# Weight remainders of three projections by an accumulating DMA in a hybrid decoder block

## The chip, the cores and the metric

The kernel runs on one core of a Trainium2 chip. The metric is the device time of one execution in microseconds (us). The engines of the core work side by side: TensorE (PE, with its weight loads as PEld), VectorE (DVE), ScalarE (ACT), GpSimd (POOL) and SyncE (SP), which in this kernel issues the transfers. Data come from HBM into SBUF, and TensorE writes its results to PSUM.

## The reference

One decoder layer on 512 tokens of width 1024, in float32. Cut to what matters:

```
h = rms_norm(x, g_pre_mix) * (1 + scale1) + shift1          # shift, scale, gate = silu(c) @ w_ada + b_ada
z = h @ w_in                                                # 2048 GLU | 384 q | 256 kv | 64 rope key | 2 x 1024 gates
u = ua * sigmoid(ub)
u = silu(layer_norm(causal_depthwise_conv(u, conv_w, conv_b)))   # 31 taps, 1024 channels
y_a = u @ w_conv_out
q, kv = rms_norm(q_lat) @ w_uq, rms_norm(kv_lat) @ w_ukv
y_b = attention(q, kv, rope) @ w_attn_out                   # 8 heads, causal
y = (sigmoid(g_a) * y_a + sigmoid(g_b) * y_b) @ w_out
x = x + gate1 * rms_norm(y, g_post_mix)
h = rms_norm(x, g_pre_mlp) * (1 + scale2) + shift2
x = x + gate2 * rms_norm(relu(h @ w_mlp_in)**2 @ w_mlp_out, g_post_mlp)
```

## The kernel before, in words

**Three matmuls for one.** TensorE multiplies in a rounded float format (fp32r). To keep float32 accuracy each factor is split into a rounded high part h and a remainder l = value - h, and a product is made of three matmuls: h*h, h*l and l*h (`mm3`). For activations the split is made as they leave PSUM. For weights, class `W` (line 470) makes it: ACT copies the float32 weights to the rounded high part, then DVE subtracts that from the weights to make the remainder.

**Weight units.** `wunit` (line 490) loads a block of weights of at most 128 x 1024 words (512 KB) from HBM into a buffer of the float arena `f_arena`, splits it into two buffers of the arena `r_arena`, and frees the float buffer. A unit of 1024 columns feeds 24 matmuls of 512 columns. Both arenas are one long SBUF tensor each (22,400 and 28,000 words per partition), in which places are given and taken back, so how far ahead weights are prepared depends on the room.

**The stages.** First the norm of x, the modulation from `w_ada`, and the first products with `w_in` (seven column blocks, whose weights go through `W` directly). Then the latents (`lat_gemm`, line 818), the rest of the GLU columns (`glu_tile`, line 898) and the latent norm; the attention, head by head; the projection `w_attn_out`, then the two gates (`C_GB`, then `C_GA`, columns of `w_in`) and `w_conv_out`, all four through `feat_gemm` (line 1152) in groups of output tiles; `w_out`, and the MLP with a Strassen scheme.

**The convolution** runs on DVE: 8 channel tiles of 31 taps, in pairs of tiles (0,1), (2,3), (4,5), (6,7). A tap is one instruction of 128 x 512 that reads the padded input and the accumulator, both in SBUF. Taps have no other consumer than the LayerNorm over channels, so they fill DVE's free time from 73 to 371 us. The LayerNorm's statistics (`ln_stats`, line 1214) begin with tiles 0 to 3: TensorE transposes them for one token tile, ACT sums them, POOL scales the sum, and ACT squares the transposed values with that as bias, after which the PSUM bank is free for the next token tile:

```
act.activation(ra.v(j), pb.v(b, n * P), AF.Copy, accum_out=sA[:, t:t + 1])
pool.tensor_scalar(ns[:, t:t + 1], sA[:, t:t + 1], -1.0 / (n * P), None, ALU.mult)
...
act.activation(ra.v(j), pb.v(b, n * P), AF.Square, bias=ns[:, t:t + 1], accum_out=q[:, t:t + 1])
```

They are recorded behind the gate `C_GB`, with a high rank for TensorE.

**The order.** Nothing is issued as it is written. A planner records all operations with their dependences, gives each an assumed cost (475 ns on the issuing engine for a DMA, then a shared DMA resource with fixed latencies), and simulates the engines: TensorE takes the ready operation of the lowest rank, every other engine the one that is due first. The order that comes out is written to the engines' queues, where each engine then works strictly in that order. The arenas' places are planned over several passes, and the pass with the shortest simulated length is taken. So a change of one operation can shift the order of others. In the profile nearly every instruction has line 388, at which the planner issues; groups are told apart by tiles.

Of the kernel before, what the change touches and what calls it, by code (L numbers as in the profile page):

```python
# [15 lines left out]
ALU = mybir.AluOpType  # L16
# [376 lines left out]
def tile_hybrid_block(  # L393
# [12 lines left out]
    out = out[0]  # L406
    w_ada, w_in, conv_w, w_conv_out = w_ada[0], w_in[0], conv_w[0], w_conv_out[0]
    w_uq, w_ukv, w_attn_out, w_out = w_uq[0], w_ukv[0], w_attn_out[0], w_out[0]
# [31 lines left out]
    def emit(past, replay):  # L440
        fa = Arena(FT, F_WORDS, past.get("f_arena"), replay.get("f_arena"))
        ra = Arena(RT, R_WORDS, past.get("r_arena"), replay.get("r_arena"))
        pb = Banks(PT, past.get("psum"), replay.get("psum"))
        plan = Planner(nc, dict(f_arena=fa, r_arena=ra, psum=pb))
        pe, act, dve, pool, sp = (plan.engine(e) for e in Planner.NAMES)

        def rf(b, pat=None, **kw):
            a = RTF[:, b[0]:b[0] + b[1]]
            return a.rearrange(pat, **kw) if pat else a
# [12 lines left out]
        def pair(words):  # L462
            return ra.alloc(words), ra.alloc(words)

        def load(words, src, pat=None, **kw):
            b = fa.alloc(words)
            sp.dma_start(out=fa.v(b, pat, **kw), in_=src)
            return b

        class W:  # L470


            def __init__(self, src, a, b):
                self.a, self.b = a, b
                self.h, self.l = pair(a * b)
                act.copy(ra.v(self.h, "p (a b) -> p a b", a=a), src)
                dve.tensor_tensor(ra.v(self.l, "p (a b) -> p a b", a=a), src,
                                  rf(self.h, "p (a b) -> p a b", a=a), ALU.subtract)

# [10 lines left out]
        def wunit(src, k0, c0, nk, nc_):  # L490

            wb = load(nk * nc_, src[k0 * P:(k0 + nk) * P, c0:c0 + nc_].rearrange("(k p) n -> p k n", p=P),
                      "p (k n) -> p k n", k=nk)
            w = W(fa.v(wb, "p (k n) -> p k n", k=nk), nk, nc_)
            fa.free(wb)
            return w

# [3 lines left out]
        def stat(n=1):  # L501
            a = st_n[0]
            st_n[0] += n
            assert st_n[0] <= 96
            return st[:, a:a + n]
# [36 lines left out]
        for t in range(NT):  # L542
            b = fa.alloc(D)
# [7 lines left out]
        for i, vecs in enumerate(((("bada", b_ada), ("gpm", g_pre_mix)),  # L551
# [5 lines left out]
            for nm, src in vecs:  # L557
                n = src.shape[1] // P
# [40 lines left out]
        for t in range(NT):  # L599
            j = ra.alloc(D)  # L600
            s = stat(2)
# [7 lines left out]
        for k in range(KD):  # L609
            b = pb.alloc()  # L610
# [77 lines left out]
        for ks in KGRP:  # L688
            plan.hurry = HA - 1e4 * ks[0]
            n = len(ks) * P  # L690
# [127 lines left out]
        def lat_gemm():  # L818
            lb = [pb.alloc() for _ in range(NT)]
            for k0 in range(0, KD, 2):  # L820
                w = wunit(w_in, k0, C_QL, 2, 512)
                for k in range(2):
                    for t in range(NT):
                        mm3(pb.v(lb[t]), hs(k0 + k, t * P, P), w(k, 0, 512), k0 + k == 0, k0 + k == KD - 1)
                w.free()
                pump(PUMPS[0])
            for t in range(NT):
                b = fa.alloc(640)
                act.copy(fa.v(b)[:, 0:512], pb.v(lb[t]))
                latF.append(b)  # L830
            pb.free(*lb)
            ws = [wunit(w_in, kh, C_R2, 4, 192) for kh in (0, 4)]
            for t in range(NT):
                b = pb.alloc()
                for k in range(KD):
                    mm3(pb.v(b, 192), hs(k, t * P, P), ws[k // 4](k % 4, 0, 192), k == 0, k == KD - 1)
                act.copy(fa.v(latF[t])[:, 512:640], pb.v(b, 128))
                act.copy(fa.v(kraw)[:, t * DR:(t + 1) * DR], pb.v(b, 192)[:, 128:192])
                pb.free(b)
            for w in ws:  # L840
                w.free()
            pump(PUMPS[0])
# [55 lines left out]
        def glu_tile(ct, s, n):  # L898

            bb = [pb.alloc() for _ in range(n)]  # L900
            for kh in range(0, KD, 4):
                w = wunit(w_in, kh, s * D + ct * P, 4, n * P)
                for o in range(n):
                    for k in range(4):
                        mm3(pb.v(bb[o]), w(k, o * P, P), hs(kh + k), kh + k == 0, kh + k == KD - 1)
                w.free()
            return bb
# [433 lines left out]
        for t in range(NT):  # L1341
            b = fa.alloc(D)
# [8 lines left out]
        for k0 in range(0, KD, 2):  # L1351
            w = wunit(w_out, k0, 0, 2, 512)
# [16 lines left out]
        for tp in range(2):  # L1369
            xn = []  # L1370
            for t in (2 * tp, 2 * tp + 1):
# [4 lines left out]
                s = stat(6)  # L1376
# [26 lines left out]
            for k2 in range(KD // 2):  # L1403
                b = pb.alloc()
                for q in range(2):
                    for t in range(2):
                        k = 2 * k2 + q
                        pe.transpose(pb.v(b)[:, (2 * q + t) * P:(2 * q + t + 1) * P], fa.v(xn[t])[:, k * P:(k + 1) * P], ident)
                for q in range(2):
                    k = 2 * k2 + q  # L1410
# [223 lines left out]
```

## Time and profile before

| what | us |
|---|---|
| median of 3 runs (lowest to highest) | 838.59 (838.47 to 839.24) |
| profiled execution | 836.4 |
| its span | 834.6 |
| PE busy | 808.1 |
| DVE busy | 685.2 |
| ACT busy | 415.5 |
| POOL busy | 45.4 |

The span is the time from the first to the last instruction; the profiled execution is 1.8 us longer. Busy times are sums over the span, and they say nothing about who waits for whom; for that the profile has a chain of waits, a timeline, and groups of instructions with the idle time before them. In a group's row stand engine, operation, what is written from what (tile names), partitions x elements and types, the count, the busy time, the mean length in ns, and the idle time before with what ended it.

### The profile page before, as it was taken

How to read it: one execution, taken by the hardware profiler on the slowest of the kernel's cores; microseconds unless marked ns; L12 is line 12 of the kernel's file. 1: busy time of each engine (PE TensorE's matmuls, PEld its weight loads, DVE VectorE, ACT ScalarE, POOL GpSimd, SP SyncE). 2: the span in 40 equal slices, each digit the busy share in tenths (PEclk: the TensorE clock that was granted, in tenths of full speed). 3: DMA queues.
4: the chain of work that ended last, by engine and by line, in shares of the span. 5: the costliest groups of instructions: out<-in, count | busy, mean ns of one | idle time of the engine just before them, and what ended most of it. 6: DMA issues, size and time to landing. Idle time of an engine off the chain costs nothing.

```text
span 834.6 us, 10659 instructions
## 1 busy us (share of the span) xinstructions
PE 808.1 (97%) x3940; PEld 675.7 (81%) x3940; DVE 685.2 (82%) x1012; ACT 415.5 (50%) x680; POOL 45.4 (5%) x119
## 2 busy tenths in 40 slices
PE   6999999999999989999999989999999999999995
PEld 3777888899988868888888779888888888888884
DVE  4979979999999997999999779298529993975696
ACT  5463363375893346227434287375346544553641
POOL 3001040000000020000000230000000000000002
PEclk9999999999999999999999989999999999999998
DMA  9997423202353141332799650064014831660302
GB/s 310 336 311 234 148 69 98 67 27 77 101 177 102 51 128 49 101 111 91 233 353 363 210 201 27 26 202 152 0 51 132 290 132 51 197 206 1 101 1 101
DMA packets 86823, 117.28 MB, mean 141 GB/s; under 512 B 7274, under 2 KB 60627, under 8 KB 86770
## 3 DMA queue, kind: packets, MB, share of 16 engines
q1 hardware_dynamic: 86770, 116.59, 43.5%
q8 instruction: 31, 0.51, 0.2%
q14 instruction: 22, 0.18, 0.1%
HBM read 108.18 MB, written 8.39 MB: 140 GB/s over the span
## 4 chain that ended last, share of the span: by engine, by line
PE 85%; DMA 4%; DVE 3%; POOL 2%; issue 2%; ACT 2%; SPq 1%; DVEq 0%; POOLq 0%; ACTq 0%
PE psum L388 85%; DMA f_arena<-in_w_in_dram 4%; DVE f_arena L388 3%; SPq L388 1%; POOL stats L388 1%; ACT f_arena L388 1%; DMA f_arena<-in_x_dram 1%; ACT r_arena L388 1%; POOL lns L388 1%; DVE r_arena L388 0%; DVEq L1629 0%; POOLq L1629 0%; DMA rows<-in_kv_norm_g_dram 0%; DVE mod L388 0%; DVE cols L388 0%
## 5 line engine op out<-in xcount | busy, mean ns | idle before, releaser
L388 PE MATMUL psum<-r_arena 128*128 128x512 f32 (+2 forms) x3592 | 766.5, 374 | 4.0 <-ACT r_arena L388 2.5
L388 PEld LDWEIGHTS psum<-r_arena 128*128 128x128 f32 x3592 | 634.4, 190 | 121.0 <-ACT r_arena L388 3.6
L388 DVE TENSOR_TENSOR r_arena<-f_arena,r_arena 128x1024 fp32r<-128x1024 f32 (+4 forms) x232 | 247.9, 1090 | 97.1 <-PE psum L388 48.5
L388 ACT CAST r_arena<-f_arena 128x1024 fp32r<-128x1024 f32 (+4 forms) x222 | 209.7, 966 | 183.3 <-PE psum L388 111.5
L388 DVE SCALAR_TENSOR_TENSOR f_arena<-f_arena,cw 128x512 f32<-128x512 f32 x240 | 164.8, 743 | 0.0
L388 ACT ACTIVATE f_arena<-psum 128x512 f32<-128x512 f32 x64 | 38.0, 597 | 119.6 <-PE psum L388 111.3
L388 DVE TENSOR_TENSOR f_arena<-f_arena 128x1024 f32<-128x1024 f32 (+3 forms) x78 | 77.0, 1003 | 8.3 <-ACT f_arena L388 6.3
L388 ACT ACTIVATE f_arena<-f_arena 128x512 f32<-128x512 f32 (+3 forms) x100 | 58.5, 604 | 20.2 <-DVE f_arena L388 19.4
L388 DVE SCALAR_TENSOR_TENSOR f_arena<-f_arena,cT 128x256 f32<-128x256 f32 (+2 forms) x84 | 55.2, 699 | 0.1
L388 PE MATMUL psum<-ident,f_arena 128*128 128x128 f32 (+1 forms) x240 | 35.3, 288 | 11.7 <-DVE f_arena L388 7.7
L388 PEld LDWEIGHTS psum<-ident,f_arena 128*128 128x128 f32 (+1 forms) x240 | 29.2, 148 | 17.2 <-DVE f_arena L388 8.7
L388 POOL TENSOR_SCALAR stats<-stats 128x1 f32<-128x1 f32 x32 | 14.8, 463 | 467.0 <-ACT r_arena L388 361.6
L388 DVE TENSOR_TENSOR f_arena<-psum,f_arena 128x512 f32<-128x512 f32 x52 | 35.2, 684 | 4.2 <-PE psum L388 3.9
L388 ACT CAST r_arena<-psum 128x512 fp32r<-128x512 f32 (+2 forms) x57 | 30.2, 566 | 15.8 <-PE psum L388 15.4
L388 DVE TENSOR_TENSOR r_arena<-psum,r_arena 128x512 fp32r<-128x512 f32 (+2 forms) x57 | 35.7, 656 | 2.2 <-ACT r_arena L388 1.9
L388 ACT COPY f_arena<-psum 128x512 f32<-128x512 f32 (+4 forms) x42 | 19.9, 500 | 23.0 <-PE psum L388 22.7
L388 ACT ACTIVATE r_arena<-f_arena 128x512 fp32r<-128x512 f32 (+3 forms) x20 | 13.0, 648 | 21.9 <-DVE f_arena L388 18.8
L388 DVE CUSTOM_DVE_ANT_0 f_arena<-psum,mask 128x128 f32<-128x128 f32 (+3 forms) x32 | 15.0, 484 | 2.5 <-PE psum L388 2.5
L388 POOL TENSOR_SCALAR lns<-lns 128x1 f32<-128x1 f32 x4 | 5.3, 1326 | 198.5 <-ACT r_arena L388 198.5
L388 POOL TENSOR_TENSOR stats<-stats,nhalf 128x1 f32<-128x1 f32 x24 | 15.2, 633 | 1.9
L388 DVE TENSOR_SCALAR f_arena<-f_arena,stats 128x1024 f32<-128x1024 f32 x8 | 6.0, 754 | 9.9 <-POOL stats L388 9.7
L388 DVE SCALAR_TENSOR_TENSOR f_arena<-f_arena 128x512 f32<-128x512 f32 (+1 forms) x18 | 13.1, 742 | 0.0
(93 smaller groups left out, 195.4 us busy)
## 6 DMA issues: line engine op xcount, KB each, us to landing
f_arena<-in_w_ada_dram SPq DMA_DIRECT2D x16, 1024.0 KB, 5.6
f_arena<-in_w_mlp_in_dram SPq DMA_DIRECT2D x32, 512.0 KB, 5.1
f_arena<-in_w_mlp_out_dram SPq DMA_DIRECT2D x32, 512.0 KB, 5.2
f_arena<-in_w_in_dram SPq DMA_DIRECT2D x28, 512.0 KB, 4.9
f_arena<-in_x_dram SPq DMA_DIRECT2D x8, 512.0 KB, 5.3
f_arena<-in_w_ada_dram SPq DMA_DIRECT2D x16, 256.0 KB, 5.7
f_arena<-in_w_ada_dram SPq DMA_DIRECT2D x8, 512.0 KB, 6.7
h_spill<-r_arena SPq DMA_DIRECT2D x16, 256.0 KB, 5.4
```

Source lines behind the costliest of these rows:

```text
L388: getattr(self.real[o.eng], o.fn)(*o.a, **o.k)
```

## The change

`W` gets a flag `by_dma`. With it, DVE's subtraction is left out. In its place ACT writes the negated weights, in the rounded format, into the remainder's buffer, and POOL issues a DMA from the float buffer to that buffer which adds what it carries to what lies there. `wunit` sets the flag where the source is `w_in`, `w_attn_out` or `w_conv_out`: 48 units, 44 of them of 1024 columns, two of 768 and two of 512. The weights of the first products, of `w_uq`, `w_ukv`, `w_out` and of the MLP are split as before.

```diff
-            def __init__(self, src, a, b):
+            def __init__(self, src, a, b, by_dma=False):
                 self.a, self.b = a, b
                 self.h, self.l = pair(a * b)
                 act.copy(ra.v(self.h, "p (a b) -> p a b", a=a), src)
+                if by_dma:
+                    act.mul(ra.v(self.l, "p (a b) -> p a b", a=a), src, -1.0)
+                    pool.dma_start(out=ra.v(self.l, "p (a b) -> p a b", a=a), in_=src, accum_op=ALU.add)
+                    return
                 dve.tensor_tensor(ra.v(self.l, "p (a b) -> p a b", a=a), src,
                                   rf(self.h, "p (a b) -> p a b", a=a), ALU.subtract)
...
-            w = W(fa.v(wb, "p (k n) -> p k n", k=nk), nk, nc_)
+            w = W(fa.v(wb, "p (k n) -> p k n", k=nk), nk, nc_, by_dma=any(src is s for s in (w_in, w_attn_out, w_conv_out)))
```

## The prediction

> **What bounds the kernel now.** I read the page's first part, the windows of 20 us, the chain that ended last, and then the timeline around the one place where the chain leaves TensorE in the stretch that the change touches.
>
> ```profile
> PE 808.1 (97%) x3940; PEld 675.7 (81%) x3940; DVE 685.2 (82%) x1012; ACT 415.5 (50%) x680; POOL 45.4 (5%) x119
> 280.00:300.00 20.00, 20.00 (x90) 16.57 (x89) 19.36 (x24) 10.27 (x12) 0.00 (x0) 1.00 0.38 108
> 300.00:320.00 20.00, 16.00 (x73) 12.73 (x72) 14.89 (x22) 8.93 (x23) 5.31 (x4) 0.91 0.25 78
> 247.31 58.80 PE psum L388 x262
> 306.90 4.63 POOL lns L388
> 312.39 69.46 PE psum L388 x312
> ...
> 312.40:320.00 7.60, 7.60 (x34) 6.19 (x34) 3.46 (x5) 5.74 (x17) 0.69 (x3) 0.78 0.26 71
> ```
>
> In the windows (the last row is one more) the columns are window and length, then busy us of PE, weight load, DVE, ACT and POOL, granted clock, DMA share and GB/s; in the chain they are start, length, and who. TensorE bounds the kernel. From 68 to 463 us, in which nearly all the changed weights are consumed, it has one break of over half a microsecond: the four idle microseconds of the 300:320 window. There the chain runs through a POOL instruction of the LayerNorm statistics. After the idle time the clock is low for a while (0.78 in the 7.6 us after it, 1.00 before), which costs another 7.6 x 0.22 = 1.7. The place is worth 5.7 us. DVE is nearly full in these windows, but TensorE does not wait for it.
>
> This is that place, in the timeline (start, length, engine, what, in brackets the idle time before and its releaser):
>
> ```profile
> 304.91 5.38 DVE L388 SCALAR_TENSOR_TENSOR f_arena<-f_arena,cw 128x512 f32<-128x512 f32 x8
> 305.85 2.54 PE L388 MATMUL psum<-r_arena 128*128 128x512 f32 x10
> 306.90 4.62 POOL L388 TENSOR_SCALAR lns<-lns 128x1 f32<-128x1 f32 x1 [191.51 <-ACT r_arena L388]
> 310.21 1.22 DVE L388 TENSOR_TENSOR r_arena<-f_arena,r_arena 128x1024 fp32r<-128x1024 f32 x1
> 312.39 0.81 PE L388 MATMUL psum<-ident,f_arena 128*128 128x128 f32 x5 [4.00 <-ACT r_arena L388]
> L388 POOL TENSOR_SCALAR lns<-lns x4: 207/240/4618, 306.9 to 318.9; 128x1 f32<-128x1 f32 x4
> ```
>
> The POOL instruction scales one number per partition, and its sisters take 0.2 us (the last row: shortest, median, longest). This one lasts 4.62 us and ends at 311.52, just after DVE's unbroken train of instructions with two SBUF inputs (convolution taps, then one weight remainder) ends at 311.43. The same happened earlier:
>
> ```profile
> 97.72 9.36 DVE L388 SCALAR_TENSOR_TENSOR f_arena<-f_arena,cw 128x512 f32<-128x512 f32 x14
> 105.42 1.71 POOL L388 TENSOR_SCALAR stats<-stats 128x1 f32<-128x1 f32 x1 [33.27 <-ACT r_arena L388]
> ```
>
> The train ends at 107.08, the POOL instruction at 107.13. So a POOL instruction that reads SBUF stands still until DVE's train breaks. It is decisive what breaks the train, and the change removes what does.
>
> **The change, part by part.** There are 48 weight units (w_in 32, attention output 8, convolution output 8); 44 have 1024 columns.
>
> Removed: 48 remainders on DVE, 44 of them of 1.22 us, some 57 us in all.
>
> ```profile
> L388 DVE TENSOR_TENSOR r_arena<-f_arena,r_arena 128x1024 fp32r<-128x1024 f32 x28 | 34.2, 1227 | 4.5 <-ACT r_arena L388 4.5
> f_arena<-in_w_ukv_dram SPq DMA_DIRECT2D x4, 512.0 KB, 4.3
> 305.00:371.00 66.00, 46.78 (x70) 0.97 0.21 64
> ```
>
> TensorE does not wait for them, so directly they are worth 0. Indirectly they move the convolution forward. The first row is DVE from 70 to 305 us: 28 remainders, of which the four of w_ukv stay, so 24 go. Inside a train each costs 1.13 us from start to start (259.44 to 260.57, below), so 27.1; their share of the waits for ACT, 24/28 of 4.5, is 3.9. DVE is 31.0 us ahead at 305.
>
> Added on ACT: 48 copies with factor -1, 44 of them at 1.06 us.
>
> ```profile
> L388 ACT ACTIVATE r_arena<-f_arena 128x1024 fp32r<-128x1024 f32 x4 | 4.2, 1056 | 2.8 <-DMA f_arena<-in_x_dram 2.8
> 64.34 1.06 ACT L388 CAST r_arena<-f_arena 128x1024 fp32r<-128x1024 f32 x1 [0.49 <-DMA f_arena<-in_w_in_dram]
> 65.30 1.56 ACT L388 ACTIVATE f_arena<-psum 128x512 f32<-128x512 f32 x3
> ```
>
> That is about 50 us on an engine at 50%: hidden, with one exception. At 57 to 66 us ACT also feeds the end of the first products, and the gate (65.30) stands behind weight copies. Up to four added copies there could delay it by 0 to 4.2 us. I take 0, since the gate has the earlier deadline.
>
> Added on POOL: 48 DMA issues, each waiting in order for its ACT copy. Behind them stand the memsets of the padded inputs, the latent norm's statistics and the four LayerNorm instructions above. No DMA of before is issued by POOL; SP's take 0.4 us, and a price matters only above 5.44 us, the spacing of the units (263.76 to 269.20 below). I take 0.
>
> Added on the DMA engines: 48 accumulating transfers.
>
> ```profile
> x_spill<-f_arena SPq DMA_DIRECT2D x4, 512.0 KB, 3.2
> f_arena<-in_w_out_dram SPq DMA_DIRECT2D x8, 512.0 KB, 6.6
> 263.76 1.05 ACT L388 CAST r_arena<-f_arena 128x1024 fp32r<-128x1024 f32 x1 [1.85 <-PE psum L388]
> 269.20 1.06 ACT L388 CAST r_arena<-f_arena 128x1024 fp32r<-128x1024 f32 x1 [3.91 <-PE psum L388]
> 264.72 0.57 ACT L388 COPY f_arena<-psum 128x512 f32<-128x512 f32 x1
> L388 ACT CAST r_arena<-f_arena 128x1024 fp32r<-128x1024 f32 x21 | 22.1, 1056 | 32.6 <-PE psum L388 32.6
> 415.62 1.05 ACT L388 CAST r_arena<-f_arena 128x1024 fp32r<-128x1024 f32 x1 [4.33 <-DMA f_arena<-in_w_conv_out_dram]
> 413.00 0.69 DVE L388 SCALAR_TENSOR_TENSOR f_arena<-f_arena,psum 128x512 f32<-128x512 f32 x1 [0.96 <-PE psum L388]
> ```
>
> Nothing of before accumulates. From below, 512 KB land 3.2 us after issue; from above I take twice 6.6, the slowest weight row, read two times: 13.2. The cover: between 252 and 345 us there are 21 casts (sixth row) for 24 units, so three units were cast before, and the cast at 263.76 is the sixth attention-output unit. The copy at 264.72 closes the second unit (at about 264.1 on TensorE), so the sixth is needed three units later, at 264.1 + 3 x 5.44 = 280.4. From the end of cast and added copy (265.9) that leaves 14.5 us, and both ends fit. At the convolution output the first group of four units ends at 413.0 + 3 x 1.36 = 417.1 (its four tiles close a quarter of 5.44 apart, and the first at 413.0), so the sixth unit is due at 422.5; its cast ends at 416.67, and with the copy 4.8 us are left. The lower price fits, the upper misses by 8.4. I take the lower: these casts wait for loads that wait for buffers, and with the convolution done earlier buffers come free earlier. An f_arena buffer is held some 4 us longer, at the same cover.
>
> **The sum.** At 305 us there were 70 taps left, 46.8 us (the row with x70, DVE's taps alone). DVE is 31.0 ahead, so the taps end at 305 + 46.8 - 31.0 = 320.8. What broke the train in before was a weight remainder waiting for its ACT copy, every 5.4 us:
>
> ```profile
> 259.44 1.22 DVE L388 TENSOR_TENSOR r_arena<-f_arena,r_arena 128x1024 fp32r<-128x1024 f32 x1
> 260.57 2.07 DVE L388 SCALAR_TENSOR_TENSOR f_arena<-f_arena,cw 128x512 f32<-128x512 f32 x3
> 316.29 1.23 DVE L388 TENSOR_TENSOR r_arena<-f_arena,r_arena 128x1024 fp32r<-128x1024 f32 x1 [4.87 <-ACT r_arena L388]
> ```
>
> At 311.4 it was the remainder of 316.29, whose cast stood behind the blocked statistics. With no remainders left DVE has only taps until 320.8. The statistics still come at about 307, since their PSUM bank comes free with the first gate tile, which TensorE's pace sets. The POOL instruction then ends at about 320.9 instead of 311.5, and TensorE, which resumes 0.87 later, at 321.8 instead of 312.4: 9.4 us lost. The low clock follows the gap as before; at a longer gap it could last longer, by nothing or by as much again (1.7), and I take nothing. Everything else counts 0. The profiled execution took 836.4 (span 834.6 and 1.8 around it), so its like is 845.8; the median of the three runs is 2.2 above it: 838.6 + 9.4 = **848.0**. The likeliest case's own range is 843 to 853 (a lead 5 us longer or shorter).
>
> **Rivals.** *POOL slips in between two taps.* The gap goes, and the low clock with it: 838.6 - 5.7 = 832.9. For it:
>
> ```profile
> 318.35 1.41 DVE L388 SCALAR_TENSOR_TENSOR f_arena<-f_arena,cw 128x512 f32<-128x512 f32 x2
> 318.89 0.27 POOL L388 TENSOR_SCALAR lns<-lns 128x1 f32<-128x1 f32 x1 [3.68 <-ACT r_arena L388]
> ```
>
> Here it got through at the seam of two taps. Against it: five seams passed at 307 to 311 and two at 105 without effect. It decides if the instruction ends before 308.4, where TensorE runs out. The Trainium skill, SBUF — State Buffer, "Who interferes with whom", says that a DVE instruction with two SBUF inputs contends with a GpSimd one that reads SBUF, and in its summary that the second to issue blocks until the first finishes; by that rule alone one tap is the longest wait, and the time would be this rival's. The 4.62 us show a wait over a whole train instead. Chance 0.25.
>
> *It waits about as long as now,* because a planned instruction that waits for TensorE breaks the train: 838.6 within 1.5. Chance 0.13.
>
> *The transfers are late.* At the upper price the convolution output waits 8.4 us: 847.0 alone, 856.4 beside the LayerNorm wait. For it, with a DMA share of 0.96 where these units are due:
>
> ```profile
> 420.00:440.00 20.00, 20.00 (x89) 16.54 (x89) 19.74 (x25) 6.85 (x9) 0.00 (x0) 1.00 0.96 358
> ```
>
> Against it: the cover of 14.5 us before. Chance 0.12.
>
> *Taps also hold up POOL's DMA issues.* Then only the units prepared by 256 are ready; the fifth is due at 264.1 + 2 x 5.44 = 275.0, and TensorE stands until the taps end at 321, some 46 us: 885. Against it: POOL's memsets, which only write, took 0.18 us for two in the middle of remainders:
>
> ```profile
> 70.34 2.52 DVE L388 TENSOR_TENSOR r_arena<-f_arena,r_arena 128x1024 fp32r<-128x1024 f32 x2
> 71.97 0.18 POOL L388 MEMSET f_arena<- 128x30 f32 x2
> ```
>
> The Trainium skill's same page says in its summary of rules that descriptor generation on GpSimd starves while DVE is in a 2x or 4x mode, and in the section named above it infers that tensor_tensor does not starve it; the trace of before has no POOL DMA that could show either. Chance 0.05.
>
> **How the numbers follow.** The forecast has 0.45, the rivals 0.25, 0.13, 0.12 and 0.05. The range reaches down to the first rival with some slack, 832.0, and up past the transfers' case to 858; outside lie the last rival and the tails. 0.2% is 1.7 us, about what a measurement of this kernel can tell from no change. Faster: the first rival and a little of the second, 0.27. Same: 0.12. Slower: the forecast, the transfers and the last rival, 0.61.
>
> **What would show it.** Right: one POOL instruction on lns of 10 to 17 us at about 307, ending with DVE's tap train; TensorE idle some 13 us there and nowhere else new; taps done near 321 instead of 371. Wrong: that instruction under 1.5 us, TensorE waiting for r_arena weights written by DMA, or POOL's DMA issues bunched at the ends of DVE's trains.

## The result, and the profile after

The changed kernel takes **869.13 us** (median of 4 runs, 868.80 to 870.14) against 838.80 of the kernel before beside it (838.47 to 839.24): a ratio of 1.0363, with an interval of 1.0345 to 1.0381. It is slower, as forecast, but by 30.3 us and not by 9.4. The profiled execution took 870.1, its span 868.4, which is 33.8 longer than before's 834.6. Of all runs in this document one, of the kernel e3 below, ran at a lower clock and took 876.4 us where its other three took 852.3 to 859.5; it is left out.

From its page, the busy times and the DMA queues (packets, MB, share of the 16 engines):

```profile
PE 813.7 (94%) x3940; PEld 678.8 (78%) x3940; DVE 634.5 (73%) x964; ACT 458.2 (53%) x728; POOL 92.4 (11%) x167
q1 hardware_dynamic: 86770, 116.59, 41.5%
q0 software_dynamic: 6912, 24.38, 14.7%
```

And the windows in which TensorE stood, in the columns of the prediction's windows:

```profile
60.00:80.00 20.00, 7.92 (x25) 5.48 (x25) 2.18 (x4) 7.79 (x11) 3.48 (x4) 0.72 1.08 255
80.00:100.00 20.00, 19.97 (x82) 16.09 (x83) 16.35 (x31) 12.04 (x15) 5.95 (x12) 0.86 1.01 244
320.00:340.00 20.00, 10.33 (x43) 8.09 (x41) 17.36 (x27) 7.61 (x17) 14.40 (x4) 0.79 0.78 200
380.00:400.00 20.00, 10.52 (x50) 8.88 (x49) 8.59 (x26) 4.76 (x14) 1.05 (x1) 0.74 0.62 180
```

DVE is relieved of 50.7 us, and TensorE is idle in three stretches instead of one. **The early break**, 11.18 us at 69, in the timeline of ACT, DVE and PE:

```profile
65.03 0.59 ACT L388 ACTIVATE f_arena<-psum 128x512 f32<-128x512 f32 x1
77.82 0.84 ACT L388 ACTIVATE r_arena<-f_arena 128x768 fp32r<-128x768 f32 x1 [12.21 <-DMA f_arena<-in_w_in_dram]
78.57 0.58 ACT L388 ACTIVATE f_arena<-psum 128x512 f32<-128x512 f32 x1
...
79.18 0.69 DVE L388 SCALAR_TENSOR_TENSOR f_arena<-f_arena,psum 128x512 f32<-128x512 f32 x1 [12.85 <-ACT f_arena L388]
79.78 0.19 DVE L388 COPY cols<-psum 128x37 f32<-128x37 f32 x1
...
80.03 0.26 PE L388 MATMUL psum<-ident,pos4f 4*128 4x4 f32 x1 [11.18 <-DVE cols L388]
```

ACT works in order. An added weight copy (77.82) waits 12.21 us for its load, and behind it stands a gate (78.57). DVE waits for that gate (79.18), and behind this in DVE's order stands the copy (79.78) for which TensorE waits. The load's row in the chain that ended last:

```profile
52.87 24.92 DMA f_arena<-in_w_in_dram
```

The DMA queues in the window from 64 to 72 us:

```profile
q0 software_dynamic: 398, 1.44, 90.0%
q1 hardware_dynamic: 403, 0.40, 17.9%
```

The load took 24.92 us. In the 8 us the engines served 398 packets of the accumulating queue and 403 of the loads' queue, one for one, but an accumulating packet is larger (3.6 KB against 1.0 in the mean) and dearer: 90.0% of the engines' time against 17.9%. (The packets' times are added up, so where packets overlap the sum can pass 100%.) So the loads got 50 GB/s.

**The LayerNorm place**, on DVE, POOL and PE:

```profile
308.88 17.99 DVE L388 SCALAR_TENSOR_TENSOR f_arena<-f_arena,cw 128x512 f32<-128x512 f32 x27
326.78 0.70 DVE L388 SCALAR_TENSOR_TENSOR f_arena<-f_arena 128x512 f32<-128x512 f32 x1
327.38 9.38 DVE L388 SCALAR_TENSOR_TENSOR f_arena<-f_arena,cw 128x512 f32<-128x512 f32 x14
...
310.90 1.80 POOL L388 DMA_DIRECT2D r_arena<-f_arena  x2 [2.02 <-ACT r_arena L388]
321.15 6.43 POOL L388 TENSOR_SCALAR lns<-lns 128x1 f32<-128x1 f32 x1 [6.07 <-ACT r_arena L388]
330.49 7.11 POOL L388 TENSOR_SCALAR lns<-lns 128x1 f32<-128x1 f32 x2
...
328.44 1.11 PE L388 MATMUL psum<-ident,f_arena 128*128 128x128 f32 x4 [5.81 <-ACT r_arena L388]
338.29 1.07 PE L388 MATMUL psum<-ident,f_arena 128*128 128x128 f32 x4 [3.86 <-ACT r_arena L388]
```

POOL's scaling now stands twice behind DVE's taps. The first ends at 327.58, 0.10 after the gate's evacuation (326.78 + 0.70) that comes between two trains of taps without idle time; the third row of POOL has two instructions, the first of 6.93 us, ending at 337.43, 0.08 after the next evacuation. TensorE is idle for 5.81 and 3.86 us, against one break of 4.00 before. POOL's DMA issues are not held: two in 1.80 us inside the train.

**The break at 387** has 9.48 us; first a row of the chain, then DVE and PE in the timeline:

```profile
377.85 9.44 DMA f_arena<-in_w_ada_dram
```

```profile
387.39 2.60 DVE L388 SCALAR_TENSOR_TENSOR f_arena<-f_arena,cT 128x1024 f32<-128x1024 f32 x2 [8.97 <-DMA f_arena<-in_w_ada_dram]
389.92 0.42 DVE L388 CUSTOM_DVE_ANT_0 f_arena<-f_arena 128x256 f32<-128x256 f32 x1
395.61 0.29 DVE L388 TENSOR_SCALAR f_arena<-ident,lns 128x128 f32<-128x128 f32 x1 [1.17 <-POOL lns L388]
...
396.00 2.26 PE L388 MATMUL psum<-f_arena,ones 128*128 128x128 f32 x9 [9.48 <-issue]
```

It is the early break's pattern on another engine: DVE's modulation waits 8.97 us for a `w_ada` load, and the LayerNorm's last steps (389.92 on) stand behind it in DVE's order. The 1 MB loads of `w_ada` land late there. In the next rows the last number is their median landing: in the whole span of the kernel before, from 355 to 388 us in the changed kernel, and in the same stretch of e6 below, where the transfers of this stage carry an eighth of their data.

```profile
f_arena<-in_w_ada_dram SPq DMA_DIRECT2D x16, 1024.0 KB, 5.6
f_arena<-in_w_ada_dram SPq DMA_DIRECT2D x4, 1024.0 KB, 9.4
f_arena<-in_w_ada_dram SPq DMA_DIRECT2D x5, 1024.0 KB, 6.6
```

### The profile page after: what moved, and what is told of

Read it like the earlier page. It is cut to its first block, busy times and chain, and to the rows that moved or that the text cites. A ratio compares the mean times of both kernels' runs of the same rounds, so it can differ in the third digit from the quotient of the medians.

```text
span 868.4 us, 10809 instructions
## 1 busy us (share of the span) xinstructions
PE 813.7 (94%) x3940; PEld 678.8 (78%) x3940; DVE 634.5 (73%) x964; ACT 458.2 (53%) x728; POOL 92.4 (11%) x167
## 3 DMA queue, kind: packets, MB, share of 16 engines
q1 hardware_dynamic: 86770, 116.59, 41.5%
q0 software_dynamic: 6912, 24.38, 14.7%
## 4 chain that ended last, share of the span: by engine, by line
PE 73%; DMA 11%; DVE 7%; POOL 3%; ACT 3%; issue 3%; DVEq 0%; POOLq 0%; ACTq 0%; SPq 0%
PE psum L388 73%; DMA f_arena<-in_w_ada_dram 7%; DVE f_arena L388 6%; DMA f_arena<-in_w_in_dram 3%; ACT r_arena L388 2%; POOL lns L388 2%; POOL stats L388 1%; ACT f_arena L388 1%; DVE r_arena L388 1%; DMA f_arena<-in_w_conv_out_dram 0%; DMA f_arena<-in_x_dram 0%; POOL r_arena L388 0%; DVEq L1633 0%; DVE mod L388 0%; POOLq L1633 0%
## 5 line engine op out<-in xcount | busy, mean ns | idle before, releaser
L388 PE MATMUL psum<-r_arena 128*128 128x512 f32 (+3 forms) x3592 | 770.8, 375 | 5.7 <-ACT r_arena L388 3.0
L388 DVE TENSOR_TENSOR r_arena<-f_arena,r_arena 128x1024 fp32r<-128x1024 f32 (+4 forms) x184 | 191.7, 1067 | 106.3 <-PE psum L388 48.7
L388 ACT ACTIVATE r_arena<-f_arena 128x1024 fp32r<-128x1024 f32 (+4 forms) x68 | 62.2, 919 | 85.5 <-PE psum L388 26.4
L388 POOL DMA_DIRECT2D r_arena<-f_arena x48 | 41.9, 876 | 322.5 <-ACT r_arena L388 263.1
L388 ACT CAST r_arena<-psum 128x512 fp32r<-128x512 f32 (+2 forms) x57 | 30.3, 568 | 9.3 <-PE psum L388 8.9
L388 DVE SCALAR_TENSOR_TENSOR f_arena<-f_arena,psum 128x512 f32<-128x512 f32 x16 | 10.8, 683 | 19.1 <-ACT f_arena L388 19.1
```

Of the source, the lines that this page charges most:

```text
L388: getattr(self.real[o.eng], o.fn)(*o.a, **o.k)
```

## The experiments

Eighteen kernels ran. Times are medians; the ratio, with its 95% interval, is to the kernel before on the same chip (its median there lay between 836.4 and 838.3).

**How much is the transfers?** Two kernels keep the changed kernel's order on every engine and alter only what the 48 transfers carry.

```diff
 # e1: at the issue, for each op with accum_op
+out=out[0:16], in_=in_[0:16]
 # e2
-pool.dma_start(out=..., in_=src, accum_op=ALU.add)
+pool.dma_start(out=..., in_=src)
```

> The order of every engine's instructions is the changed kernel's; each accumulating transfer carries 16 of the 128 partitions, an eighth of its data, so seven eighths of those remainders are left as the negated weights. Theory (the loss is the transfers' share of the DMA engines): the breaks of 11.18 us at 69 and 9.48 us at 387 go, with most of the low clock behind them, and the two of 5.81 and 3.86 us behind the blocked POOL instruction stay: 869.1 - 11.2 - 9.5 - about 3 = 845, from 842 to 850. Rival (the planner's other order, ACT's added copies or POOL's issues cost it, whatever the transfers carry): 869 within 3.

> As the changed kernel in the order of every engine, but the 48 transfers copy and do not add, so the remainders of those units hold the whole weights. Theory a (adding is dear: 24.38 MB in 14.7% of the 16 engines' span, 2.66 us of all engines for 512 KB, against 1.62 for the loads): a plain copy takes less, the breaks at 69 and 387 shrink by about half, 855 to 862. Theory b (a second stream of 24 MB costs that much whether it adds or not): 869 within 3.

e1 took 844.3 (1.0062, 1.0039 to 1.0085): the breaks at 69 and 387 are gone (0.94 us is left at 373), those at the LayerNorm stayed with 5.81 and 3.45 us. e2 took 853.6 (1.0179, 1.0163 to 1.0195), with breaks of 3.07 at 69 and 2.84 at 379. Its queue on the page:

```profile
q0 software_dynamic: 6912, 24.38, 7.9%
```

The same bytes as plain copies need 7.9% of its span of 852.7, that is 67.4 us of all engines, against 127.7 when they add (14.7% of 868.4). So adding nearly doubles the engines' time, as theory a of e2 has it, and plain copies gain more than it gave: the breaks shrink by over two thirds, and the time is 1.4 us under its range. Theory b fails, though a second stream that does not add still costs. By the ratios, of 30.4 us (3.63% of some 838) some 15.4 are the adding (1.0363 to 1.0179), 9.8 the second stream as such (to 1.0062), and 5.2 remain when the transfers carry an eighth.

**Is each break made by its own transfers?** Again in the changed kernel's order, with thin transfers (an eighth of the data) for the 16 units ahead of the attention (e5) or for the second gate and the convolution output (e6); e13 leaves the transfers and sets an unread word behind every tap.

```diff
 # e5, e6: as e1, for units 0 to 15, or 32 to 47
 # e13: behind each tap, at the issue
+self.real["dve"].memset(junk, 0.0)
```

> The changed kernel's order on every engine; the accumulating transfers of the 16 units of w_in ahead of the attention carry an eighth of their data (their other remainders stay the negated weights), the 32 later ones carry all. Theory (each break has its own transfers): the break of 11.18 us at 69 goes with the low clock behind it, the others stay: 869.1 - 11.2 - 3 = 855, from 852 to 859; the one at 387 still 7 to 11 us. Rival (one lateness at the start carries through, and the break at 387 is its consequence): 845, with both gone.

> The same, with the 16 units of the second gate and the convolution output thin and the 32 ahead of them whole. Theory: the break of 9.48 us at 387 goes with its low clock (0.74 in its 20 us), the one of 11.18 at 69 stays: 869.1 - 9.5 - 3 = 857, from 853 to 861. Rival (the break at 387 comes from LayerNorm statistics that end late, not from the transfers of that stage): 866 to 870.

> The changed kernel in its own order; behind each tap DVE sets one unread word per partition to zero, which in the kernel before let POOL through at once. Theory (three separate breaks): the two of 5.81 and 3.86 us go with some 2.5 of low clock, the ones at 69 and 387 stay: 857, from 854 to 860. Rival (the break at 387 is the consequence of the LayerNorm's delay): it goes too, 845 to 848.

e5: 857.3 (1.0234, 1.0206 to 1.0262); the break at 69 is gone, one of 9.70 at 372 remains. e6: 859.9 (1.0269, 1.0251 to 1.0288); 12.78 remain at 67, the break at 387 is gone. e13: 860.2 (1.0279, 1.0258 to 1.0299), 0.2 past the edge of its range; the LayerNorm's breaks are gone, and 12.31 at 67 and 10.41 at 375 remain. Each break went with its own cause and left the others standing. By the ratios they are worth 1.29%, 0.94% and 0.84%, together 25.7 of the 30.4 us. Each of these differences is uncertain by some 0.3%; the rest is not assigned. The two that are the transfers' come to 18.7 us, against 25.2 in e1, which makes the 16 units in between thin too.

**The transfers late only.** The early 16 units by DVE again:

```diff
-by_dma=any(src is s for s in (w_in, w_attn_out, w_conv_out))
+by_dma=by_dma    # True in the calls for w_attn_out, C_GB, C_GA, w_conv_out
```

> The 16 units of w_in ahead of the attention go back to DVE's subtraction; the attention output, both gates and the convolution output stay with the transfers. Theory: the break of 11.18 us at 69 and the low clock behind it (0.72 and 0.86 in two windows of 20 us) go, some 14 us; DVE loses 16 x 1.2 = 19 us of its lead, so its tap train lasts longer at the LayerNorm statistics, which can give back 0 to 10: 855 to 865. Rival (the early break is only moved, since another transfer or copy is late instead): 869 within 3.

Its ratio is 1.0219 (1.0173 to 1.0265), with runs of 852.3 to 859.5, two of the three inside the theory's range. The early break is gone; TensorE is idle 6.12 at 306, 4.43 at 365 and 6.01 at 443, in an order that is no longer the changed kernel's; the POOL scalings take under 1 us there, so the first of these is not theirs. Its trace has the early break's pattern again: a gate on ACT (311.83) stands behind a weight copy (310.88) that waits 8.13 us for its `w_in` load, and that load took 16.27 us. So in part the break was moved, as the rival has it. This was read and not tested; the cause of the 4.43 was not followed.

**The LayerNorm's scaling off POOL, or POOL let in.**

```diff
 # e4 (changed kernel), e8 (kernel before)
-pool.tensor_scalar(ns[:, t:t + 1], sA[:, t:t + 1], -1.0 / (n * P), None, ALU.mult)
+act.mul(ns[:, t:t + 1], sA[:, t:t + 1], -1.0 / (n * P))
 # e12: the kernel before in its own order, with e13's memset
```

> The changed kernel with the LayerNorm's scaling by -1/512 on ACT in place of POOL. Theory: the breaks of 5.81 and 3.86 us, in which POOL stood behind DVE's tap train, go with about 2.5 us of low clock: 857, from 853 to 862 since the order changes with it. Rival (TensorE would have waited there in any case, for the statistics' other steps or for weights): 866 to 870.

> The kernel before with the scaling by -1/512 on ACT in place of POOL, and no transfer. Theory (POOL stood behind DVE's tap train for 4.0 us, and the clock was low for 1.7 more): 838.3 - 5.7 = 832.6, from 831 to 835. Rival (the bank of PSUM comes free no earlier, because ACT takes the scaling behind other work): 837 to 840.

> The kernel before in its own order, with the scaling still on POOL; behind each of the 248 taps DVE sets one word per partition to zero, which nothing reads. Theory (POOL stands still because no instruction of another kind parts DVE's taps): the POOL instruction at 307 takes under 1.5 us instead of 4.62, and TensorE's four idle microseconds there go: 832 to 835. Rival (only idle time of DVE lets POOL in): 4 us or more on POOL as before, 837 to 842.

e4: 850.3 (1.0148), more than the theory gave, since in its new order the break at 387 went too (0.84 left), while the early one stayed with 12.06; by e13 that break does not follow from the LayerNorm's. e8: 832.6 (0.9943, 0.9927 to 0.9959), as expected. Its window at the LayerNorm place has no idle TensorE and the full clock:

```profile
300.00:320.00 20.00, 20.00 (x102) 16.30 (x100) 19.32 (x28) 14.38 (x39) 0.00 (x0) 1.00 0.29 79
```

e12: 831.9 (0.9941, 0.9921 to 0.9960), with this group of POOL's (shortest, median and longest in ns), and these rows of DVE's timeline:

```profile
L388 POOL TENSOR_SCALAR lns<-lns x4: 283/500/902, 308.6 to 314.8; 128x1 f32<-128x1 f32 x4
```

```profile
304.65 0.75 DVE L388 SCALAR_TENSOR_TENSOR f_arena<-f_arena,cw 128x512 f32<-128x512 f32 x1
304.68 0.06 DVE L390 MEMSET junk<- 128x1 f32 x1
305.32 0.75 DVE L388 SCALAR_TENSOR_TENSOR f_arena<-f_arena,cw 128x512 f32<-128x512 f32 x1
305.35 0.06 DVE L390 MEMSET junk<- 128x1 f32 x1
```

The longest of the four POOL instructions takes 0.90 us instead of 4.62. The taps still start 0.67 apart, so the memsets cost nothing.

**ACT's copies alone.**

```diff
-pool.dma_start(out=l, in_=src, accum_op=ALU.add)
+dve.tensor_tensor(l, src, rf(l), ALU.add)
```

> ACT's negated copy as in the change, but DVE adds the weights to it and no transfer is made. Theory (ACT's added copies are hidden): 838.6, from 836 to 842, the remainders one ACT copy later than before. Rival (the gate behind the copies at 57 to 66 us costs up to 4.2 us, or the later remainders make TensorE wait): 842 to 850.

e7 took 835.2 (0.9978, 0.9962 to 0.9993), 0.8 under the theory's range: the copies cost nothing. That it is a little faster goes with another order, in which the break of 4.00 at the LayerNorm is 1.69.

**Is it the planner's wrong price, or the place of the gate?** In e9 and e10 the planner is told the price; in e14 a dependence holds certain weight copies back behind the third gate; e17 adds e13's memset to that.

```diff
 # e9, e10 (e10 with e4's edit)
-            return 475.0, 2000.0
+            return (880.0 if "accum_op" in k else 475.0), 2000.0
...
-            o.dma = b
+            o.dma = b * (2.0 if "accum_op" in k else 1.0)
 # e14, e17: fourth latent unit, units of 768 columns, later GLU units
+plan.after = gate
 w = W(...)
+plan.after = None
```

> The changed kernel, but the planner is told what the trace shows of an accumulating transfer: 880 ns on POOL, and 2.9 us of the shared DMA resource for 512 KB in place of 1.46. Theory (the planner believed loads to be early that the transfers make late, and put their copies in front of the gate in ACT's order): the break of 11.18 us at 69 shrinks to under 4, 850 to 860. Rival (the DMA engines lack the room, whatever the order): 866 to 870.

> The same with the scaling by -1/512 on ACT, which took the changed kernel from 869.1 to 850.3. Theory (then neither an early break nor the LayerNorm's is left): 836 to 842. Rival (the early break stays): 848 to 852.

> The changed kernel, where ACT's copies of the fourth latent unit, of the two units of 768 columns and of the later GLU units wait for the third gate by a dependence, so that no copy of a starved load stands in front of the gates. Theory a (the transfers starve the loads, but it is ACT's order that stops TensorE, which has weights ready): the break at 69 falls from 11.18 to under 3 us, 853 to 859. Theory b (TensorE lacks the weights too): it is only moved, 8 us or more at 70 to 100, 866 to 872.

> The gates ahead as in the run of 859.5, and DVE sets its unread word behind each tap. Theory: the POOL instruction of 16.89 us falls under 1.5, and the breaks of 7.26 at 133 and 5.12 at 334 go with some low clock: 844, from 841 to 848; the one of 5.63 at 450 is the transfers' and stays. Rival (the latent norm and the statistics are then held up by late transfers): 854 or more.

e9: 848.5 (1.0138), 1.5 us under the theory's range, and for a reason that was not the theory's. The early break stayed, at 12.60, with the gate again behind a copy that waits 12.65 for its load; the breaks at the LayerNorm and at 387 went with the new order, in which POOL's four scalings took 0.47 to 0.79 us between DVE's taps, without any memset. e10: 847.8 (1.0128), the rival; its early break has 12.85. e14: 859.5 (1.0281, 1.0255 to 1.0307), half a microsecond past theory a's range, but its mechanism: TensorE runs without a break over 0.4 from 63 to 133. It had its weights, and ACT's order was what stopped it. But then:

```profile
94.37 19.30 DVE L388 SCALAR_TENSOR_TENSOR f_arena<-f_arena,cw 128x512 f32<-128x512 f32 x29
...
96.82 16.89 POOL L388 TENSOR_SCALAR stats<-stats 128x1 f32<-128x1 f32 x1 [2.74 <-ACT r_arena L388]
...
140.03 2.50 PE L388 MATMUL psum<-r_arena 128*128 128x512 f32 x5 [7.26 <-DVE f_arena L388]
```

In the statistics of the latent norm a POOL instruction stands 16.89 us behind some 25 of these taps, and TensorE is idle 7.26 later. e17, 846.1 (1.0097, 1.0078 to 1.0117), confirms it: that instruction takes 0.56 us, and the breaks at 133 and 334 are gone. What is left above two microseconds reads as the transfers': 4.27 at 355, where a gate on ACT stands behind a copy that waits 6.12 us for its `w_conv_out` load, and this one at the convolution output, where TensorE waits for a remainder itself:

```profile
442.27 1.22 PE L388 MATMUL psum<-r_arena 128*128 128x512 f32 x2 [5.51 <-DMA r_arena<-f_arena]
```

**Is any of it worth having?** With the scaling on ACT, the transfers for the attention output alone (e11, and e16 beside e15 on one chip), and for the first gate too (e18).

```diff
 # e11, e16, e18: with e8's edit
+feat_gemm(w_attn_out, ..., by_dma=True)
+feat_gemm(w_in, C_GB, ..., by_dma=True)    # e18 alone
 # e15: e8 again
```

> The scaling on ACT as in the run of 832.6, and of the 48 units only the eight of the attention output by the transfers, where the DMA engines have room (share 0.38 at 280 to 300 us). Theory (TensorE bounds there, and the work taken from DVE is worth nothing): 832.6, from 831 to 834. Rival 1 (a lighter DVE helps where TensorE waits behind it): under 831. Rival 2 (the transfers delay loads even there): 835 to 842.

> The kernel before with the scaling on ACT, beside the next on one chip: 0.994 of the kernel before, as it was.

> The same with the attention output's eight units by the transfers. Theory (work taken from DVE is worth nothing where TensorE bounds): the same as without, within 1 us. Rival (it is worth the 2 us that the first runs, on two chips, seemed to show): 0.3% under it.

> The scaling on ACT, and the attention output's and the first gate's 16 units by the transfers. Theory (room on the DMA engines until about 345 us): 830.1 as with eight units, from 829 to 832. Rival (from the second eight on they collide with the loads of the second gate and of w_ada): 834 to 842.

e11: 830.3 (0.9919, 0.9904 to 0.9934), in its rival 1's range. e15: 831.7 (0.9940, 0.9925 to 0.9956). e16: **830.1** (0.9920, 0.9904 to 0.9936), the fastest version, which beats both kernels. e18: 832.3 (0.9934, 0.9918 to 0.9950), just past its theory's range and under its rival's. The 1.6 us between e15 and e16 are more than the theory's 1 and less than the rival's 2.5, and the two intervals overlap; the profiles show 3.66 us of idle TensorE at 484 in e15 and 1.69 at 483 in e16, in the end of `w_out`, so it may be the order there and not DVE's relief. This was only read, not tested. With sixteen units nothing is gained over none.

## Why the prediction was wrong

**The step that failed is the price of the transfers.** I priced one as a latency, 3.2 to 13.2 us, held it against the cover of the unit that needs it, and took the lower end as hidden. The latency lay inside these bounds (median 8.3, below), and at the two places that I examined TensorE was not held up by a remainder. What I did not price is the engines' time that a transfer takes from other transfers. Of the DMA issues from 50 to 80 us, the nine `w_in` loads (the last number is the median landing), in the kernel before:

```profile
f_arena<-in_w_in_dram SPq DMA_DIRECT2D x9, 512.0 KB, 8.8
```

and in the changed kernel, with the transfers of its whole span below:

```profile
f_arena<-in_w_in_dram SPq DMA_DIRECT2D x9, 512.0 KB, 20.9
...
r_arena<-f_arena POOLq DMA_DIRECT2D x44, 512.0 KB, 8.3
```

The window from 60 to 80 us of the kernel before had a DMA share of 0.81:

```profile
60.00:80.00 20.00, 18.36 (x82) 14.04 (x82) 17.87 (x29) 9.33 (x13) 3.65 (x8) 1.00 0.81 256
```

That row was there to read, and I quoted only later ones, up to 0.96. In e1, with the changed kernel's order and thin transfers, the same nine loads land in 10.8 us in the median. Undoing it bit by bit (e1, e2) puts some 25 us on this term, which I had at 0.

The Trainium skill, DMA: Bandwidth & Descriptors, "Queues, rings and completion order", says that each engine goes round its queues packet by packet. The 398 and 403 packets agree with equal turns, though no run here shows that the profile's packet is the page's, which has some 9 to 17 descriptors. Equal turns leave little to the queue with the cheap packets, which is what the 90.0% and 17.9% show.

**The gate behind ACT's copies** (0 to 4.2 us, taken as 0): the place was the right one to suspect, and the price of the copies was right (e7: no loss). The bound was wrong, because I counted only the copies' own length and not the wait of the first of them for a load.

**The LayerNorm term** (+9.4): the mechanism held in the changed kernel. e12 and e13 show it directly, since they add nothing but the memsets, and e14's 16.89 us is the long wait that I forecast, at another place. It was not sure to hold, and in part this was luck: in the orders of e3 and e9 all of POOL's scalings got in between taps, as the first rival had it (the last section has the rows). The size was off: with the transfers thin (e1) the two breaks sum to 9.26 us, 5.3 over the 4.00 of before, and the time is 0.62% or 5.2 us over. The step that failed here is "DVE has only taps until 320.8": I overlooked the gate's own evacuations on DVE (326.78 and 336.65 above), which come in between the taps, and POOL got in behind them; there are two waits of 6.4 and 6.9 us, not one of 10 to 17. The lead was roughly right: in e1, where nothing is late, the last tap ends at 323.0 (forecast 320.8); in the changed kernel at 336.8, after the early break.

**What was counted at nothing and is nothing:** DVE's relief in itself (but for the open 1.6 us between e15 and e16), and POOL's issues (0.88 us each, and not held by taps, so the rival of 885 is refuted). **The transfers' rival** named the right actor with the wrong victim, the remainder's reader and not the other loads. Its wait at the convolution output, forecast at 8.4 us, came in e3, e14 and e17 (6.01, 5.63 and 5.51, each with a transfer into `r_arena` as its releaser), where the early break was gone.

## What to carry to other kernels

Work moved to the DMA engines is priced twice: as a latency against its cover, and as engine time against every load that is in flight beside it, and there the stretch's DMA share is the row to read first. A load that comes late costs what stands behind its reader in an in-order queue, which may be something that never needed the load. And an idle engine's tiny instruction can be the critical one: moving four POOL scalings to ACT, or parting DVE's taps with an unread word, was worth more than 48 remainders.

## What the chip showed that I had not expected

A small POOL instruction can wait for a whole train of DVE instructions with two SBUF inputs (4.62, 6.43, 6.93, 16.89 us), past some 25 seams between them in the longest case. A memset of one word per partition behind each tap, 0.06 us long, lets it in (0.28 to 0.90 us in e12) and costs DVE nothing. But the wait does not always come. In e3, without memsets, twelve taps of a train and POOL's four scalings (shortest, median, longest in ns), of which those at 319.92 and 323.56 lie wholly inside these taps, read:

```profile
318.39 8.05 DVE L388 SCALAR_TENSOR_TENSOR f_arena<-f_arena,cw 128x512 f32<-128x512 f32 x12
L388 POOL TENSOR_SCALAR lns<-lns x4: 608/807/955, 314.4 to 323.6; 128x1 f32<-128x1 f32 x4
```

In e9 it was the same for all four, and in e14 POOL got in between taps at 318.28 and 324.94 (0.62 and 0.22 us) and stood for 5.73 at 332.64.

The Trainium skill, SBUF — State Buffer, "Who interferes with whom", speaks of a block for the whole instruction. The waits under 1 us in e3 and e9 agree with that, one or two taps long; the longer ones show a block that ended with idle time of DVE, or behind a gate's evacuation, which has two SBUF inputs as the taps do and the next tap right behind it. With the memsets, in the same orders, none lasted over 0.94 us (e12, e13, e17). Why one seam opens and another does not, no run told.

An accumulating transfer within SBUF took 127.7 / 24.38 = 5.2 us of all 16 engines per MB, the same as a plain copy 2.8, and the transfers of SP's queue, mostly loads, 41.5% of 868.4 over 116.59 MB, which is 3.1.
